# Second mixer: the weights' exact rests move from GpSimd to VectorE, and the skip is added straight out of PSUM

## The chip, the core and the metric

The kernel runs on one core of a Trainium2 chip. The metric is the device time of one execution in microseconds (us). The engines are called as in the profile: PE is TensorE (PEld its weight loads), DVE is VectorE, ACT is ScalarE, POOL is GpSimd, SP is SyncE, which issues nearly all DMAs.

## The reference, cut to what matters

Two decoder layers run one after the other on 512 tokens of width 1024. The change lies in the mixer of the second layer, a Mamba-2 state-space mixer with 32 heads of 64 channels in 4 groups:

```python
def mamba2_mixer(h, norm, w_in, conv_w, conv_b, dt_bias, a_log, d_skip, gnorm, w_out):
    proj = rms_norm(h, norm) @ w_in              # z | x,B,C | dt
    xbc = silu(causal_depthwise_conv(xbc, conv_w, conv_b))
    ...
    y = ssd_chunked(xf * dt[..., None], dt * A, b_in, c_in)   # inside a chunk + from the states
    y = y + xf * d_skip.astype(f32)[:, None]                  # the skip
    y = y.reshape(b, s, SSM_INNER) * silu(z)
    y = y * rsqrt(mean(y * y over a group) + eps) * gnorm
    return y @ w_out
```

## The kernel before

**Three passes for every product.** Weights and activations are float32. Each weight tile `wraw` (128 x 1024 values, one DMA of 512 KB) is split into a rounded part `whi` (a copy on ScalarE) and the exact rest `wlo = wraw - whi` (a `tensor_tensor` subtraction). A product is then three matmuls: `xh,whi`, `xl,whi` and `xh,wlo` (`mm3`). Which engine makes the rest is set by the list `lo_turns`, from which `wload3` takes turns: `[V]` is VectorE, `[G]` is GpSimd. The second mixer sets it to `[G]` at L1482 and back to `[V]` at L1728, before its last output product. There are two buffers each of `wraw`, `whi` and `wlo`, so a weight tile's DMA waits until an earlier tile's rest is made, and a rounded half waits until the matmuls are done with the one two tiles before.

**The second mixer.** `odd_mixer` works by groups of 8 heads. The generator `core(g, ...)` does a group's scan in steps; `weave` spreads the dense products (`dq`: the next group's projections, the previous group's output product, and for the last group the keys and values of the memory, `mem_kv`) evenly between its steps. A dense product of one weight tile is a "job" of 24 matmuls into one of three PSUM buffers `lin`; its `sink` takes the result out of PSUM: `pd` and then three multiply-adds and a gate into `xf`, `Bt`, `Ct` for the convolutions, or `z` for the gates, or an addition to `hT` for outputs.

In `core`, for each of four pairs of heads `hp`: `pst` (PSUM, one buffer) gets the states' part of chunks 1 to 3; `seg` is made by ScalarE (decays) and multiplied with `CB` on VectorE; `py` (PSUM) gets the part inside the chunks from `seg`; VectorE puts `y` together and multiplies it into `zs[hp]`. `ecums[hp]` holds the decays with which `pst` is scaled; it is a tile `ecumB` with two buffers, loaded by two DMAs on SP's queue in `cum_load`. After the four pairs, `gss` collects the sum of squares (added on GpSimd), and VectorE multiplies the four `z` with it and makes the split halves `oyh`, `oyl` for the output product.

**What sets the order.** The program is written in one order, and a scheduler then sets each engine's own order from a simulated timeline. Each engine runs its list strictly in that order. The changed program goes through the same scheduler.

Of the kernel before, what the change touches and what calls it, by code (L numbers as in the profile page):

```python
# [15 lines left out]
ALU = mybir.AluOpType  # L16
# [4 lines left out]
P = 128  # L21
T = 512
# [57 lines left out]
def kernel(ctx: ExitStack, tc: tile.TileContext, a: dict, out: bass.AP, stage: str = "exfoXF"):  # L80
    nc = tc.nc
    V, S, G, TE = nc.vector, nc.scalar, nc.gpsimd, nc.tensor
# [12 lines left out]
    def nm(s):  # L95
        uid[0] += 1
        return f"{s}_{uid[0]}"
# [12 lines left out]
    def ps(tag="ps", n="", w=512):  # L110
        p_, tags = next(c for c in reversed(cur) if tag in c[1])
        return p_.tile([P, w], F32, tag=tag, name=nm(n or tag), bufs=tags[tag])
# [3 lines left out]
    def mm(o, l, r, start, stop, **kw):  # L116
        last_mm[0] = TE.matmul(o, l, r, start=start, stop=stop, **kw)  # L117
# [3 lines left out]
    def act(o, i, f, scale=1.0, bias=0.0, **kw):  # L121
        ins = S.activation(o, i, f, scale=scale, bias=bias, **kw)  # L122
        if f in (AF.Silu, AF.Tanh, AF.Sin):
            switch.append(ins)
        return ins

    def logs():

        with ExitStack() as es:
            for ins in switch:  # L130
                es.enter_context(tc.issue_after(ins.ins))
            S.preload_act_table_set(LNS)
        switch.clear()

    def tt(e, o, x, y, op):
        return e.tensor_tensor(o, x, y, op=op)  # L136

    def stt(o, x, sc, y, op0, op1):
        return V.scalar_tensor_tensor(o, x, sc, y, op0=op0, op1=op1)  # L139
# [38 lines left out]
    lo_turns = [V]  # L178
# [43 lines left out]
    dcol = cp.tile([P, 16], F32, name="dcol")  # L222
# [102 lines left out]
    def rsq(o, src, scale, bias):  # L325
        act(o, src, AF.Ln, scale=scale, bias=bias)
        act(o, o, AF.Exp, scale=-0.5)
# [1151 lines left out]

    def odd_mixer():  # L1480
        win = a["od_w_in"][0]
        lo_turns[:] = [G]  # L1482
        wout = a["od_w_out"][0]
        INNER = 2048
        NC = T // P
# [6 lines left out]
        with pool("odd") as op, pool("oddram", space=DRAM) as dp, \  # L1492
                psum(lin=3, pc=2, py=2, ps2=1):
            xh, xl, R, fin = prenorm(xp, colr("od_norm", 8), tag="py")
            t_ = lambda tag, shape, bufs=1, dt=F32: op.tile(list(shape), dt, tag=tag, name=nm(tag), bufs=bufs)
# [102 lines left out]
            def core(g, d, zs, res):  # L1598
                Bt, Ct, xf = d["B"], d["C"], d["xf"]
                EL = t_("EL", (P, HG, NC), 2)  # L1600
                nc.sync.dma_start(EL, edram[g * HG:(g + 1) * HG, :].partition_broadcast(P))
                cums, ecums = [], []

                def cum_load(hp):
                    h0 = g * HG + hp * 2
                    cumB = t_("cumB", (P, 2, T), 2)
                    nc.sync.dma_start(cumB, cdram[h0:h0 + 2, :].partition_broadcast(P))
                    cums.append(cumB)
                    ecumB = t_("ecumB", (P, T - P), 2)
                    for j in range(2):  # L1610
                        nc.sync.dma_start(ecumB[j * 64:(j + 1) * 64, :], xdram[h0 + j, P:T].partition_broadcast(64))
                    ecums.append(ecumB)

                cum_load(0)
                BT = t_("BT", (P, NC, P))
                pt = ps("pc", "odd_m_pt2")
                for c in range(NC):
                    TE.transpose(pt[:, c * P:(c + 1) * P], Bt[:, c * P:(c + 1) * P], ident)
                act(BT.rearrange("p c n -> p (c n)"), pt, AF.Copy)
                CB = t_("CB", (P, NC, P))  # L1620
                pt = ps("pc", "odd_m_pt3")
                for c in range(NC):
                    cs = slice(c * P, (c + 1) * P)
                    mm(pt[:, cs], Bt[:, cs], Ct[:, cs], True, True)
                tt(V, CB, pt.rearrange("p (c l) -> p c l", c=NC), smask.unsqueeze(1).to_broadcast([P, NC, P]), ALU.mult)
                yield
                xdt = [t_(f"xdt{c}", (P, 512)) for c in range(NC)]
                sts = [None] * NC
                for c in range(NC):
                    cs = slice(c * P, (c + 1) * P)  # L1630
                    pt = ps("pc", "odd_m_pt4")
                    for i in range(4):
                        TE.transpose(pt[:, i * P:(i + 1) * P], xf[i][:, cs], ident)  # L1633
                    hb = lambda j: tms[:, j, c, g * HG:(g + 1) * HG].unsqueeze(2).to_broadcast([P, HG, 64])
                    ptv = pt.rearrange("p (h d) -> p h d", d=64)
                    tt(V, xdt[c].rearrange("p (h d) -> p h d", d=64), ptv, hb(0), ALU.mult)
                    if c < NC - 1:
                        xe = t_("xe", (P, 512), 2)
                        tt(V, xe.rearrange("p (h d) -> p h d", d=64), ptv, hb(2), ALU.mult)
                        pS = ps("pc", "odd_m_pS5")  # L1640
                        mm(pS, BT[:, c, :], xe, True, True)
                        st = t_(f"st{c}", (P, 512))
                        if c == 0:
                            act(st, pS, AF.Copy)
                        else:
                            eb = EL[:, :, c].unsqueeze(2).to_broadcast([P, HG, 64])
                            tt(G, st.rearrange("p (h d) -> p h d", d=64), sts[c].rearrange("p (h d) -> p h d", d=64),
                               eb, ALU.mult)
                            tt(V, st, st, pS, ALU.add)
                        sts[c + 1] = st  # L1650
                    yield
                ss = t_("gss", (P, T))
                for hp in range(4):

                    hs2 = slice(hp * P, (hp + 1) * P)
                    pst = ps("ps2", "odd_m_ps8")
                    for c in range(1, NC):
                        mm(pst[:, c * P:(c + 1) * P], sts[c][:, hs2], Ct[:, c * P:(c + 1) * P], True, True)
                    y = t_("y", (P, T), 2)
                    dc = dcol[:, g * 4 + hp:g * 4 + hp + 1]  # L1660
                    tt(V, y[:, P:T], pst[:, P:T], ecums[hp], ALU.mult)
                    V.tensor_scalar(y[:, 0:P], xf[hp][:, 0:P], dc, None, op0=ALU.mult)
                    stt(y[:, P:T], xf[hp][:, P:T], dc, y[:, P:T], ALU.mult, ALU.add)
                    py = ps("py", "odd_m_py6")
                    if hp < 3:
                        cum_load(hp + 1)
                    for j in range(2):
                        hl = hp * 2 + j
                        h = g * HG + hl
                        cB = cums[hp][:, j, :]  # L1670
                        sg = t_("seg", (P, NC, P), 2)
                        for c in range(NC):
                            act(sg[:, c, :], cB[:, c * P:(c + 1) * P], AF.Relu, scale=-1.0, bias=tms[:, 1, c, h:h + 1])
                        act(sg, sg, AF.Exp, scale=-1.0)
                        tt(V, sg, sg, CB, ALU.mult)
                        q2 = slice(j * 64, j * 64 + 64)
                        hs = slice(hl * 64, hl * 64 + 64)
                        for c in range(NC):
                            mm(py[q2, c * P:(c + 1) * P], xdt[c][:, hs], sg[:, c, :], True, True)
                        yield  # L1680
                    tt(V, y, y, py, ALU.add)
                    tt(V, zs[hp], y, zs[hp], ALU.mult)
                    if hp == 0:
                        act(ss, zs[hp], AF.Square)
                    else:
                        sq = t_("y", (P, T), 2)
                        act(sq, zs[hp], AF.Square)
                        tt(G, ss, ss, sq, ALU.add)
                yield
                pr = ps("pc", "odd_m_pr7")  # L1690
                mm(pr, ones, ss, True, True)
                Rg = t_("gss", (P, T))
                logs()
                rsq(Rg, pr, 1.0 / 512, eps_c)
                yield
                yh, yl = [], []
                for hp in range(4):
                    tt(V, zs[hp], zs[hp], Rg, ALU.mult)
                    h_ = t_(f"oyh{hp}", (P, T), dt=F32R)
                    l_ = t_(f"oyl{hp}", (P, T), dt=F32R)  # L1700
                    split(h_, l_, zs[hp], col("ssm_gnorm", g * 4 + hp))
                    yh.append(h_)
                    yl.append(l_)
                res.extend((yh, yl))
                yield
# [53 lines left out]
    if "o" in stage:  # L1759
        mem = odd_mixer()  # L1760
# [51 lines left out]
```

## Time and profile before

| | |
|---|---|
| time, median of 3 runs | 1826.12 us (1825.3 to 1826.51) |
| profiled execution | 1823.81 us, its span 1822.0 us |
| busy in the span | PE 96%, PEld 76%, DVE 61%, ACT 41%, POOL 21% |
| granted TensorE clock, mean | 0.978 of 2.4 GHz |

The span runs from the first to the last instruction of the profiled execution; 1.8 us lie around it. Busy time of PE counts matmuls from issue to modelled end, and they overlap, so PE counts as busy while one follows the other; what is read below is where PE is *not* busy and what ended that wait. The mixer of the second layer lies between about 930 and 1380 us of the span.

### The profile page before, as it was taken

To read this page: it belongs to the slowest core of one execution; us is meant where nothing else is said; L and a number is where in the kernel's file an instruction comes from. 1 tells how busy PE (TensorE), PEld (TensorE's weight loads), DVE (VectorE), ACT (ScalarE), POOL (GpSimd) and SP (SyncE) were. 2 spreads that over 40 slices of the span, in tenths; PEclk is the share of its full clock that TensorE was granted. 3 is DMA by queue.
4 is the path that set the end of the run, shared out by engine and by line. 5 is a ranking of instruction groups with operands and counts; after the bars stand their busy time and mean duration, and the time that the engine had idled before them with its cause. 6 is when DMAs were issued, how large, how long until landed. Compare 5 with 4: busy or idle time off the path is not lost. (4 is left out here: it accounts for less than half of the span.)

```text
span 1822.0 us, 25550 instructions
## 1 busy us (share of the span) xinstructions
PE 1746.2 (96%) x10192; PEld 1385.7 (76%) x10192; DVE 1111.7 (61%) x1662; ACT 741.5 (41%) x1273; POOL 382.1 (21%) x265
## 2 busy tenths in 40 slices
PE   7899999999899999999998998999989999999998
PEld 5667767777677888888875766777777788888886
DVE  6586677757566444343476979688776754443543
ACT  3443454455444223132354645454544432222322
POOL 6222211211312100001253344334341100000000
PEclk9899989999999999999999999999999999999999
DMA  5232101012212333333333423233332133323332
GB/s 158 70 90 83 48 19 29 21 59 82 81 35 93 94 103 94 98 97 95 93 93 105 122 80 122 71 118 97 90 116 70 47 104 95 102 93 100 97 93 93
DMA packets 171869, 157.15 MB, mean 86 GB/s; under 512 B 12075, under 2 KB 150182, under 8 KB 171750
## 3 DMA queue, kind: packets, MB, share of 16 engines
q1 hardware_dynamic: 169574, 155.51, 28.3%
q8 instruction: 80, 1.31, 0.3%
q14 instruction: 39, 0.32, 0.1%
q10 hardware_dynamic: 2176, 0.01, 0.1%
HBM read 150.90 MB, written 4.59 MB: 85 GB/s over the span
## 5 line engine op out<-in xcount | busy, mean ns | idle before, releaser
L122 ACT ACTIVATE whi<-wraw 128x1024 fp32r<-128x1024 f32 (+1 forms) x255 | 265.8, 1042 | 589.6 <-PE lin L117 498.6
L117 PE MATMUL lin<-xh,whi 128*128 128x512 f32 x1192 | 475.0, 401 | 10.8 <-ACT whi L122 5.0
L117 PE MATMUL lin<-xl,whi 128*128 128x512 f32 x1192 | 472.1, 397 | 1.0 <-DVE xl L139 1.0
L117 PE MATMUL lin<-xh,wlo 128*128 128x512 f32 x1192 | 453.9, 397 | 1.7 <-POOL pd L1553 1.2
L136 DVE TENSOR_TENSOR wlo<-wraw,whi 128x1024 fp32r<-128x1024 f32 (+1 forms) x158 | 193.9, 1227 | 339.5 <-ACT whi L122 339.2
L136 POOL TENSOR_TENSOR wlo<-wraw,whi 128x1024 fp32r<-128x1024 f32 x97 | 237.9, 2453 | 598.2 <-ACT whi L122 589.7
L117 PEld LDWEIGHTS lin<-xh,whi 128*128 128x128 f32 x1192 | 226.0, 190 | 63.6 <-issue 8.7
L117 PEld LDWEIGHTS lin<-xh,wlo 128*128 128x128 f32 x1192 | 225.5, 189 | 54.2 <-issue 2.4
L117 PEld LDWEIGHTS lin<-xl,whi 128*128 128x128 f32 x1192 | 225.8, 189 | 52.2 <-issue 2.1
L136 DVE TENSOR_TENSOR hT<-hT,lin 128x512 f32<-128x512 f32 x160 | 107.8, 684 | 82.9 <-PE lin L117 82.1
L117 PE MATMUL lin<-gl,whi 128*128 128x512 f32 x352 | 137.3, 390 | 0.5 <-DVE gl L136 0.5
L117 PE MATMUL lin<-gh,whi 128*128 128x512 f32 x352 | 136.2, 391 | 0.0
L117 PE MATMUL lin<-gh,wlo 128*128 128x512 f32 x352 | 125.7, 389 | 0.0
L136 DVE TENSOR_TENSOR s<-lin,R 128x512 f32<-128x512 f32 x88 | 60.0, 690 | 52.3 <-PE lin L117 52.3
L117 PEld LDWEIGHTS lin<-gl,whi 128*128 128x128 f32 x352 | 66.1, 188 | 14.4 <-DVE gl L136 0.9
L117 PEld LDWEIGHTS lin<-gh,wlo 128*128 128x128 f32 x352 | 66.1, 188 | 13.7
L117 PEld LDWEIGHTS lin<-gh,whi 128*128 128x128 f32 x352 | 66.1, 188 | 13.5
L122 ACT ACTIVATE s<-s 128x512 f32<-128x512 f32 x44 | 27.4, 624 | 69.0 <-DVE s L136 69.0
L122 ACT ACTIVATE seg<-cumB,tms 128x128 f32<-128x128 f32 x128 | 40.3, 390 | 31.0 <-PE odd_m_py L117 30.6
L117 PE MATMUL lin<-oyh,wlo 128*128 128x512 f32 x128 | 50.3, 398 | 1.7 <-DVE wlo L136 1.7
L117 PE MATMUL lin<-oyh,whi 128*128 128x512 f32 x128 | 51.8, 405 | 0.1
L117 PE MATMUL lin<-oyl,whi 128*128 128x512 f32 x128 | 51.2, 400 | 0.0
(440 smaller groups left out, 2854.3 us busy)
## 6 DMA issues: line engine op xcount, KB each, us to landing
wraw<-in_ffn_w_dram SPq DMA_DIRECT2D x176, 256.0 KB
wraw<-in_ffn_w_dram SPq DMA_DIRECT2D x44, 512.0 KB
wraw<-in_od_w_in_dram SPq DMA_DIRECT2D x41, 512.0 KB
wraw<-in_ev_w_in_dram SPq DMA_DIRECT2D x17, 512.0 KB
wraw<-in_xa_wkv_dram SPq DMA_DIRECT2D x16, 512.0 KB
cumB<-cdram SPq DMA_DIRECT2D x16, 512.0 KB
wraw<-in_od_w_out_dram SPq DMA_DIRECT2D x16, 512.0 KB
wraw<-in_ev_w_out_dram SPq DMA_DIRECT2D x8, 512.0 KB
```

The lines of the kernel that those rows point to most:

```text
L117: last_mm[0] = TE.matmul(o, l, r, start=start, stop=stop, **kw)
L122: ins = S.activation(o, i, f, scale=scale, bias=bias, **kw)
L136: return e.tensor_tensor(o, x, y, op=op)
```

## The change

Two edits, both in the second mixer. `lo_turns` is set to `[V]`, so that the 61 rests of this mixer that GpSimd made are made by VectorE (all but its last output product's, which VectorE made already). And `y` is put together in another way: before, `pst` was scaled into `y`, the skip (`xf` times a column of `dcol`) was written to `y`'s first chunk and added to the other three, and `py` was added. Now `pst` is scaled in place into the `ecumB` tile (`yst`), `y` is made in one step from `xf`, the column and `py` straight out of PSUM, and `yst` is added to chunks 1 to 3. That is three VectorE instructions per pair in place of four, and `y` is taken from its pool only after `py`.

```diff
     def odd_mixer():
         win = a["od_w_in"][0]
-        lo_turns[:] = [G]
+        lo_turns[:] = [V]
         wout = a["od_w_out"][0]
...
-                    y = t_("y", (P, T), 2)
-                    dc = dcol[:, g * 4 + hp:g * 4 + hp + 1]
-                    tt(V, y[:, P:T], pst[:, P:T], ecums[hp], ALU.mult)
-                    V.tensor_scalar(y[:, 0:P], xf[hp][:, 0:P], dc, None, op0=ALU.mult)
-                    stt(y[:, P:T], xf[hp][:, P:T], dc, y[:, P:T], ALU.mult, ALU.add)
+                    yst = ecums[hp]
+                    tt(V, yst, pst[:, P:T], yst, ALU.mult)
                     py = ps("py", "odd_m_py6")
...
-                    tt(V, y, y, py, ALU.add)
+                    y = t_("y", (P, T), 2)
+                    stt(y, xf[hp], dcol[:, g * 4 + hp:g * 4 + hp + 1], py, ALU.mult, ALU.add)
+                    tt(V, y[:, P:T], y[:, P:T], yst, ALU.add)
                     tt(V, zs[hp], y, zs[hp], ALU.mult)
```

Three places of VectorE's list show how the scheduler placed the rests. The first is the end of group 0's scan: `z<-z,gss` scales the four gates, `oyl` are the output's rests, and the last row takes the next group's first gate product out of a `lin` buffer. Before:

```order
L139 SCALAR_TENSOR_TENSOR xf_1618_8652<-pd_9282,colt,xf_1618_8652 128x512 x3
L139 SCALAR_TENSOR_TENSOR xf_1618_8652<-th_9289,xf_1618_8652 128x512
L136 TENSOR_TENSOR z_1609_8643<-z_1609_8643,gss_9214 128x512
L136 TENSOR_TENSOR z_1610_8644<-z_1610_8644,gss_9214 128x512
L136 TENSOR_TENSOR z_1611_8645<-z_1611_8645,gss_9214 128x512
L136 TENSOR_TENSOR z_1612_8646<-z_1612_8646,gss_9214 128x512
L139 SCALAR_TENSOR_TENSOR oyl_1730_9246<-z_1609_8643,colt,oyh_1729_9245 128x512
L139 SCALAR_TENSOR_TENSOR oyl_1732_9251<-z_1610_8644,colt,oyh_1731_9250 128x512
L139 SCALAR_TENSOR_TENSOR oyl_1734_9256<-z_1611_8645,colt,oyh_1733_9255 128x512
L139 SCALAR_TENSOR_TENSOR z_1739_9292<-lin_9337,R_8256 128x512
```

The same place on VectorE in the changed kernel:

```order
L136 TENSOR_TENSOR wlo_9379<-wraw_9331,whi_9378 128x1024
L139 SCALAR_TENSOR_TENSOR xf_1618_8652<-pd_9278,colt,xf_1618_8652 128x512
L139 SCALAR_TENSOR_TENSOR xf_1618_8652<-th_9285,xf_1618_8652 128x512
L136 TENSOR_TENSOR wlo_9427<-wraw_9382,whi_9426 128x1024
L136 TENSOR_TENSOR z_1609_8643<-z_1609_8643,gss_9210 128x512
L136 TENSOR_TENSOR z_1610_8644<-z_1610_8644,gss_9210 128x512
L136 TENSOR_TENSOR z_1611_8645<-z_1611_8645,gss_9210 128x512
L136 TENSOR_TENSOR z_1612_8646<-z_1612_8646,gss_9210 128x512
L139 SCALAR_TENSOR_TENSOR oyl_1730_9242<-z_1609_8643,colt,oyh_1729_9241 128x512
L139 SCALAR_TENSOR_TENSOR oyl_1732_9247<-z_1610_8644,colt,oyh_1731_9246 128x512
L139 SCALAR_TENSOR_TENSOR oyl_1734_9252<-z_1611_8645,colt,oyh_1733_9251 128x512
L139 SCALAR_TENSOR_TENSOR z_1739_9288<-lin_9333,R_8256 128x512
```

Two rests now stand ahead of the four scalings; the second one waits for a rounded half that ScalarE can write only when PE is done with the job two tiles before.

The second place is group 1's third and fourth pair on VectorE, where `seg` must be ready for PE's next `py`. Before:

```order
L136 TENSOR_TENSOR y_9755<-y_9755,odd_m_py_1837_9759 128x512
L136 TENSOR_TENSOR z_1741_9294<-y_9755,z_1741_9294 128x512
L136 TENSOR_TENSOR y_9875<-odd_m_ps_1855_9871,ecumB_9762 128x384
L1662 TENSOR_SCALAR y_9875<-xf_1618_8652,dcol 128x128
L136 TENSOR_TENSOR pd_9897<-lin_9847,R_8256 128x512
L139 SCALAR_TENSOR_TENSOR y_9875<-xf_1618_8652,dcol,y_9875 128x384
L139 SCALAR_TENSOR_TENSOR xf_1747_9300<-th_9838,xf_1747_9300 128x512
L136 TENSOR_TENSOR seg_9880<-seg_9880,CB_9316 128x512
L136 TENSOR_TENSOR hT_76<-hT_76,lin_9913 128x512
L136 TENSOR_TENSOR seg_9934<-seg_9934,CB_9316 128x512
```

The same place in the changed kernel:

```order
L136 TENSOR_TENSOR wlo_9898<-wraw_9836,whi_9897 128x1024
L139 SCALAR_TENSOR_TENSOR y_9857<-xf_1617_8651,dcol,odd_m_py_1836_9750 128x512
L139 SCALAR_TENSOR_TENSOR xf_1748_9297<-pd_9887,colt,xf_1748_9297 128x512
L136 TENSOR_TENSOR hT_76<-hT_76,lin_9903 128x512
L136 TENSOR_TENSOR y_9857<-y_9857,ecumB_9631 128x384
L139 SCALAR_TENSOR_TENSOR xf_1748_9297<-pd_9887,colt,xf_1748_9297 128x512
L139 SCALAR_TENSOR_TENSOR xf_1747_9296<-th_9829,xf_1747_9296 128x512
L136 TENSOR_TENSOR seg_9870<-seg_9870,CB_9312 128x512
L136 TENSOR_TENSOR z_1741_9290<-y_9857,z_1741_9290 128x512
L136 TENSOR_TENSOR seg_9924<-seg_9924,CB_9312 128x512
```

The fourth pair's skip is gone from the rows ahead of its `seg`; the third pair's sum out of `py`, two convolution steps and a rest have come there.

The third place is the chain of the memory's keys on VectorE: `nv`, `nt`, `nt`, `rk`, `k` is one key's norm, each from the one before. Before:

```order
L318 TENSOR_SCALAR nv_11545<-mem_k_pr_2187_11543 128x256
L136 TENSOR_TENSOR nt_11546<-rk_11540 128x256
L139 SCALAR_TENSOR_TENSOR nt_11546<-nt_11546,nv_11545 128x256
L139 SCALAR_TENSOR_TENSOR rk_11540<-nt_11546,rk_11540 128x256
L318 TENSOR_SCALAR nv_11597<-mem_k_pr_2198_11595 128x256
L139 SCALAR_TENSOR_TENSOR k_2146_11364<-kf_11538,gk_11367,rk_11540 128x256
```

And in the changed kernel:

```order
L318 TENSOR_SCALAR nv_11527<-mem_k_pr_2186_11525 128x256
L136 TENSOR_TENSOR wlo_11635<-wraw_11594,whi_11634 128x1024
L139 SCALAR_TENSOR_TENSOR k_2145_11347<-kf_11473,gk_11350,rk_11475 128x256
L136 TENSOR_TENSOR nt_11528<-rk_11522 128x256
L139 SCALAR_TENSOR_TENSOR nt_11528<-nt_11528,nv_11527 128x256
L139 SCALAR_TENSOR_TENSOR rk_11522<-nt_11528,rk_11522 128x256
L136 TENSOR_TENSOR wlo_11673<-wraw_11638,whi_11672 128x1024
L139 SCALAR_TENSOR_TENSOR k_2145_11347<-kf_11520,gk_11350,rk_11522 128x256
```

One rest stands in each key's chain now.

## Rows read from the trace of the kernel before

**Rows 1.** Stretches: us, then busy us (x count) of PE, PEld, DVE, ACT, POOL; PEclk, DMA share, GB/s.
```profile
600.00:900.00 300.00, 300.00 (x1325) 248.55 (x1324) 121.53 (x149) 82.72 (x96) 23.91 (x10) 1.00 0.32 97
...
940.00:1000.00 60.00, 51.54 (x222) 39.29 (x220) 45.16 (x55) 28.83 (x44) 20.05 (x15) 0.94 0.36 105
...
1060.00:1075.00 15.00, 10.46 (x46) 8.40 (x45) 12.21 (x15) 8.33 (x12) 4.88 (x2) 0.89 0.13 36
...
1120.00:1142.00 22.00, 16.08 (x76) 12.51 (x76) 19.61 (x21) 11.07 (x22) 8.72 (x6) 0.84 0.34 105
...
1318.00:1360.00 42.00, 35.08 (x236) 31.04 (x235) 32.43 (x39) 20.44 (x40) 21.77 (x10) 0.96 0.37 108
...
1000.00:1320.00 320.00, 309.04 (x1479) 241.34 (x1478) 257.86 (x311) 165.79 (x299) 129.60 (x75) 0.98 0.34 100
```

**Rows 2.** Waits of PE from 930 to 1380 us: us in total, times, longest us.
```profile
PE odd_m_py L117 <- DVE seg L136: 7.9, 4, 4.5
PE lin L117 <- DVE z L139: 4.5, 1, 4.5
PE odd_m_py L117 <- DVE xdt L136: 3.5, 1, 3.5
PE mem_k_pr L117 <- ACT ksq L122: 2.2, 2, 1.9
...
PE lin L117 <- DVE wlo L136: 1.7, 1, 1.7
PE lin L117 <- POOL pd L1553: 1.2, 1, 1.2
```

**Rows 3.** VectorE's groups, 940 to 1360 us: count | busy us, mean ns | idle before.
```profile
L139 DVE SCALAR_TENSOR_TENSOR xf<-pd,colt,xf 128x512 f32<-128x512 f32 x48 | 47.8, 1011 | 2.2 <-ACT xf L122 1.7
L136 DVE TENSOR_TENSOR seg<-seg,CB 128x512 f32<-128x512 f32 x32 | 36.3, 1148 | 3.6 <-ACT seg L122 3.6
L139 DVE SCALAR_TENSOR_TENSOR z<-th,z 128x512 f32<-128x512 f32 x16 | 27.9, 1747 | 9.8 <-ACT th L122 9.8
L139 DVE SCALAR_TENSOR_TENSOR y<-xf,dcol,y 128x384 f32<-128x384 f32 x16 | 23.2, 1451 | 0.0
L136 DVE TENSOR_TENSOR z<-z,gss 128x512 f32<-128x512 f32 x16 | 17.5, 1154 | 5.3 <-ACT gss L122 5.3
...
L139 DVE SCALAR_TENSOR_TENSOR z<-lin,R 128x512 f32<-128x512 f32 x16 | 11.0, 685 | 12.5 <-PE lin L117 8.9 <-DMA xdram<-z 3.5
...
L1662 DVE TENSOR_SCALAR y<-xf,dcol 128x128 f32<-128x128 f32 x16 | 8.9, 558 | 0.0
L136 DVE TENSOR_TENSOR y<-odd_m_ps,ecumB 128x384 f32<-128x384 f32 x16 | 8.8, 549 | 0.8 <-PE odd_m_ps L117 0.6
```

**Rows 4.** GpSimd and VectorE instructions in order of time: start us, us, engine, operation.
```profile
1132.98 2.79 POOL L136 TENSOR_TENSOR wlo<-wraw,whi 128x1024 fp32r<-128x1024 f32 x1
1133.49 2.82 DVE L136 TENSOR_TENSOR seg<-seg,CB 128x512 f32<-128x512 f32 x1
...
1330.63 2.40 POOL L136 TENSOR_TENSOR wlo<-wraw,whi 128x1024 fp32r<-128x1024 f32 x1 [0.67 <-ACT whi L122]
1330.73 2.57 DVE L139 SCALAR_TENSOR_TENSOR rk<-nt,rk 128x256 f32<-128x256 f32 x1
```

**Rows 5.** GpSimd's groups, 940 to 1360 us, columns as in group 3.
```profile
L136 POOL TENSOR_TENSOR wlo<-wraw,whi 128x1024 fp32r<-128x1024 f32 x56 | 140.0, 2500 | 137.2 <-ACT whi L122 128.8 <-PE odd_m_pt L1633 6.0 <-PE odd_m_ps L117 2.3
L136 POOL TENSOR_TENSOR gss<-gss,y 128x512 f32<-128x512 f32 x12 | 18.2, 1519 | 18.8 <-ACT y L122 18.8
L136 POOL TENSOR_TENSOR st<-st,EL 128x512 f32<-128x512 f32 x8 | 8.5, 1062 | 22.4 <-ACT st L122 11.8 <-DVE st L136 10.7
```

**Rows 6.** VectorE's rests in the first FFN, 640 to 900 us, columns as in group 3.
```profile
L136 DVE TENSOR_TENSOR wlo<-wraw,whi 128x1024 fp32r<-128x1024 f32 x40 | 48.9, 1224 | 122.5 <-ACT whi L122 122.5
```

**Rows 7.** SP's queue from 930 to 1380 us, waits: us in total, times, longest us.
```profile
SPq L1611 <- DVE y L136: 29.5, 7, 6.6
```

## Prediction

> **What bounds the kernel now.** I read first how the span splits into stretches. In the first FFN PE is busy for all of 300 us at a granted clock of 1.00 [rows 1]: nothing that VectorE does there costs time. In the second mixer PE is short of work in four places: 60.00 − 51.54 = 8.5 us from 940 to 1000, 4.5 from 1060 to 1075, 5.9 from 1120 to 1142 and 6.9 from 1318 to 1360, 25.8 us together [rows 1]. The granted clock falls there too. A stretch of t us at a mean clock c does work that full clock would do in c·t, so the clock costs 60 × 0.06 = 3.6, 15 × 0.11 = 1.7, 22 × 0.16 = 3.5 and 42 × 0.04 = 1.7, together 10.5 us. So 36 us is the most that this change can bring: all else is PE at work.
>
> Second, the list of what PE waits for between 930 and 1380 us: nearly all names VectorE (`seg` 7.9 us, `z` 4.5, `xdt` 3.5) [rows 2]. In the same stretches VectorE is busy 75 to 89% of the time (19.61 of 22 us from 1120 to 1142) [rows 1].
>
> Third, why VectorE is late: its instructions of one size have very different times [rows 3]. A 128x512 step out of PSUM, `z<-lin,R`, takes 685 ns; the same size with both inputs in SBUF takes 1011 (`xf`), 1148 (`seg`), 1154 (`z` by `gss`) or 1747 (`z<-th`). For 128x384, `y<-odd_m_ps,ecumB` out of PSUM takes 549 and the skip's step, all SBUF, 1451. Put in order of time, GpSimd and VectorE show the reason: `seg` starts 0.5 us into a GpSimd rest of 2.79 us and ends 0.54 us after it, that is, it runs its own time once the rest is over; a `rk` of half the size, started 0.1 us into a rest of 2.40, ends 0.27 after it [rows 4]. VectorE stands still while GpSimd reads.
>
> The Trainium skill, page "SBUF — State Buffer", section "Who interferes with whom", says the same: a VectorE instruction with two SBUF inputs and a GpSimd one that reads SBUF share a port that is locked for a whole instruction, and "Issue order, not op shape, decides who blocks". By that last sentence the moved rests would in turn hold GpSimd's remaining steps; that rival is weighed below by its rows.
>
> **The change part by part.** *Holds removed.* Excess over the PSUM forms [rows 3]: `xf` 48 × (1.011 − 0.685) = 15.6 us, `seg` 32 × 0.463 = 14.8, `z<-th` 16 × 1.062 = 17.0, the skip's step 16 × 0.902 = 14.4, `z` by `gss` 16 × 0.469 = 7.5: 69 us. GpSimd is busy with rests for 140.0 us of 166.7 in this stretch, the others being `gss` 18.2 and `st` 8.5 [rows 5], so 84%, 58 us, should go with the rests. Bounds: nothing, if the times are those of the forms and not of GpSimd (but `seg` and `xf` are of one size and differ, and [rows 4] shows ends tied to GpSimd's), and all 69.
>
> *Rests added.* A VectorE rest takes 1224 ns in the FFN [rows 6]; the 56 of this stretch [rows 5] make 68.5 us, the 61 of the mixer 75.
>
> *The sum of `y`.* Removed are 8.9 us (skip of the first chunk) and 23.2 us (its step on three) [rows 3], of which 14.4 are already counted as holds. The sum with `py` stays one step out of PSUM, now with the skip in it; the trace has no such form of three operands except `z<-lin,R` of 685 ns, which I take for it (bounds: 16 × (±0.2), 3 us). Added is a 128x384 step with both inputs in SBUF: 549 if free of GpSimd, 1451 if held as today; I take 549, 8.8 us, since the rests go. Net −8.9 − 8.8 + 8.8 = −8.9 us.
>
> So VectorE's load changes by −58 + 68.5 − 8.9 = +1.6 us of some 340: **no relief on average**. What changes is where it is. A hold of up to 2.8 us falls on whatever VectorE has next; where it is always busy, nearly the whole rest of 2.5 us is lost for each GpSimd rest, and in its place stands a step of 1.22 us. I go by stretch.
>
> 940 to 1000: the `xdt` wait (3.5) and `pd` (1.2) hang on held `z<-th` and `xf` steps. One `z<-th` hold of 1.1 and two or three `xf` of 0.33 lie in each such chain: I take 3 of 8.5 us.
>
> 1060 to 1075, the end of a group: the four scalings lose 4 × 0.47 = 1.9 us of holds, `xf` steps ahead of them some 2; by the order shown above, two rests have come ahead of the scalings, of which one, 1.22, comes out of this chain's time. Gain 3 of 4.5.
>
> 1120 to 1142: VectorE-bound over the two pairs before (`seg` waits, the longest 4.5 [rows 2]). Two pairs have four `seg` (1.9 us of holds), two skip steps (1.8) and `y`'s own saving (2 × 8.9/16 = 1.1), some six `xf` (2.0) and three `z<-th` (3.2): 10 us out, four rests in, 4.9. Gain 5 of 5.9.
>
> 1318 to 1360, the keys: each key's chain has a hold of about 2 us (`rk`, 2.57 us, ends 0.27 after the rest [rows 4]) and by the order gets one rest of 1.22 in its place; the last group's `seg` and scalings lose 1.5 + 1.9. I take 4 of 6.9.
>
> Sum 15 of 25.8 us. The clock comes back in proportion, 15/25.8 × 10.5 = 6 us; it was 0.84 where PE idled most and 1.00 where it never did [rows 1].
>
> *New waits.* VectorE now stands at a rest until `whi` is there, and `seg`, `xf`, `y` are queued behind it. Below: 0, as in the FFN, where VectorE sat idle 122.5 us ahead of 40 rests for `whi` [rows 6] and PE was never short. Above: the four stretches are 139 us of 420, so about 20 rests lie in them, each at 1.7 us, PE's one wait for a VectorE rest [rows 2]: 34 us. I take three waits of 1.7, one for each of the three stretches where VectorE is the engine waited for, 5 us, since elsewhere the FFN is the nearer row.
>
> *Moved.* The `ecumB` buffer is now free only after `yst` is added. The load that reuses it is issued by SP, which stands 29.5 us for it today, 7 times, up to 6.6 [rows 7], and none of PE's longer waits is for it [rows 2]; a pair takes over 20 us (16 pairs in some 380), so I cost it at nothing. Without that cover it would cost what lies between the two steps: about a rest, five 512 steps and a 384 step, 1.22 + 5 × 0.685 + 0.55 = 5.2 us, once a group, 21 us.
>
> Total −15 − 6 + 5 = −16 us: 1823.8 becomes 1807.8 for an execution like the profiled one, which lies 2.3 us below the median; so about 1810.
>
> **The rivals.** *Half comes back.* If holds only hide behind ScalarE (`th` 9.8 us, `seg` 3.6, `gss` 5.3 of VectorE's own waits [rows 3]), PE gets 7 or 8 us and with a little clock, less new waits, −8: 1818.
>
> *All comes back*: −36 to −30, 1790 to 1796. VectorE's unchanged mean load speaks against it.
>
> *GpSimd held in turn.* The 12 `gss` additions run on GpSimd at 1519 ns [rows 5]; if each rest on VectorE holds one up by its 1.22, the last of each group is on the chain to the scalings: 4 × 1.2 = 5 us, and 1815. This is what issue order deciding, in the Trainium skill's section named above, would give; no row of before shows a VectorE rest beside a GpSimd step. I count it within the forecast's range.
>
> *`ecumB` late*: the 21 us above; at 16 it eats the gain. Up to 1831. Against it: a whole pair's time as cover.
>
> *Slower: VectorE, in order, stands at its rests.* GpSimd idled 128.8 us for `whi` ahead of 56 rests, 2.3 us each [rows 5], and nobody was behind it. From 1000 to 1320 VectorE has 320 − 257.86 = 62 us free [rows 1] for some 43 of the rests, 1.44 us each: **from a mean standing time of 1.44 us on, VectorE is full** and becomes the bound. At 2.3 it lacks 43 × 0.86 = 37 us, less the 16 of gain: 1845. For it: the second rest ahead of the scalings waits for a job that PE has yet to finish. Against it: GpSimd idled because it was free early; a busy engine comes to a rest when `whi` has long been there.
>
> *The holds are not GpSimd's doing.* Then 68.5 us of rests come on top, 43 × 1.22 = 53 of them from 1000 to 1320, VectorE at 303 of 320 after `y`'s saving of 7.5: about 1835. [rows 4] speaks against it.
>
> **How the numbers follow.** Of 1826, 0.2% is 3.7 us, about what a measurement of this kernel can tell from no change: faster is below 1822.5. Forecast with its own range 1798 to 1815: 0.60. Half: 0.21. All: 0.05. `ecumB` late: 0.05, shared between no change and slower. VectorE standing: 0.06. No holds to remove: 0.03. Faster is 0.60 + 0.21 + 0.05 less 0.02 for the edge of the half case, 0.84; no change 0.02 + 0.03 = 0.05; slower 0.02 + 0.06 + 0.03 = 0.11. The range from 1796 to 1823 leaves out the slower cases and most of the full return.
>
> **What would show it.** Right: `xf`, `seg` and `z<-z,gss` near 0.7 us, `z<-th` under 1; VectorE's busy time within a few us of before, GpSimd's near 27 from 940 to 1360; PE's waits for `seg`, `z` and `xdt` together under 8 us; clock in 1120 to 1142 above 0.9. Wrong: VectorE idle for `whi` above 60 us with PE waits for `seg` behind it; `xf` still near 1 us; PE waiting for the states' loads.

## The result and the profile after

The changed kernel takes 1805.64 us (median of 5 runs, 1798.9 to 1808.38) against 1826.12: the ratio is 0.9887, with a 95% interval of 0.9868 to 0.9906. The forecast was 1810 us and a range from 1796 to 1823. The profiled execution took 1798.9 us, the shortest of the five; its span is 1797.1.

Single executions differ by some us ahead of the change already. The first FFN ends at 918.7 us in the trace of before and at 916.8 in the one after, with nothing changed until then; over the runs below that point lies between 916.7 and 923.3. So beside the medians I compare the length of **the second mixer in the trace**, from the end of the first FFN's last addition to `hT` to the end of the last but one of this mixer's: 1375.2 − 918.7 = 456.5 us before, 1350.9 − 916.8 = 434.2 after. Those 22.3 us answer to the 20.5 of the medians; the rest of the program is as long as before within a few us.

VectorE's groups after the change, from 940 to 1336 us (the same part of the program as in [rows 3]; columns as there):

```profile
L136 DVE TENSOR_TENSOR wlo<-wraw,whi 128x1024 fp32r<-128x1024 f32 x58 | 72.4, 1248 | 8.4 <-ACT whi L122 5.7 <-PE lin L117 2.3
L139 DVE SCALAR_TENSOR_TENSOR xf<-pd,colt,xf 128x512 f32<-128x512 f32 x46 | 37.6, 823 | 1.7 <-ACT xf L122 1.6
L136 DVE TENSOR_TENSOR seg<-seg,CB 128x512 f32<-128x512 f32 x32 | 21.1, 685 | 0.0
...
L139 DVE SCALAR_TENSOR_TENSOR y<-xf,dcol,odd_m_py 128x512 f32<-128x512 f32 x16 | 11.9, 745 | 7.4 <-PE odd_m_py L117 7.4
L139 DVE SCALAR_TENSOR_TENSOR z<-th,z 128x512 f32<-128x512 f32 x16 | 11.8, 740 | 0.4 <-ACT th L122 0.4
...
L136 DVE TENSOR_TENSOR z<-z,gss 128x512 f32<-128x512 f32 x16 | 10.0, 687 | 3.1 <-ACT gss L122 3.1
...
L136 DVE TENSOR_TENSOR ecumB<-odd_m_ps,ecumB 128x384 f32<-128x384 f32 x16 | 8.9, 554 | 2.0 <-PE odd_m_ps L117 1.9
L136 DVE TENSOR_TENSOR y<-y,ecumB 128x384 f32<-128x384 f32 x16 | 8.8, 552 | 0.1
```

`seg` fell from 1148 ns to 685, `z<-th` from 1747 to 740, `z` by `gss` from 1154 to 687, `xf` from 1011 to 823: what looked like slow forms in [rows 3] were mostly holds, that is, time in which the step stands still beside a GpSimd step. GpSimd has these reading steps left:

```profile
L136 POOL TENSOR_TENSOR gss<-gss,y 128x512 f32<-128x512 f32 x12 | 20.0, 1666 | 103.6 <-ACT y L122 103.6
L136 POOL TENSOR_TENSOR st<-st,EL 128x512 f32<-128x512 f32 x8 | 9.0, 1131 | 108.3 <-ACT st L122 81.1 <-DVE st L136 27.2
```

The stretches of [rows 1], now at the places where PE is as far in its work as at 940, 1000, 1060, 1075, 1120, 1142, 1318 and 1360 us before (columns as there):

```profile
938.00:997.00 59.00, 50.97 (x222) 39.39 (x221) 43.91 (x62) 29.74 (x45) 2.73 (x8) 0.91 0.34 99
1055.50:1068.50 13.00, 10.69 (x46) 8.51 (x45) 10.69 (x17) 7.20 (x11) 0.00 (x0) 0.87 0.15 42
1113.30:1125.70 12.40, 12.40 (x66) 10.06 (x65) 12.37 (x19) 8.52 (x17) 1.98 (x3) 1.00 0.45 144
1299.00:1335.80 36.80, 33.91 (x236) 30.35 (x236) 28.70 (x46) 21.77 (x42) 3.34 (x2) 0.95 0.42 126
```

The third row is the plainest: 22 us at a clock of 0.84, with PE waiting for `seg`, have become 12.4 us of PE without a gap at 1.00. The first has hardly changed.

These places are worked out from the starts of the matmuls in both traces: each counts as much as its kind's median distance to the next start in the trace of before, and times at which the sums are equal belong together. The same sums tell where the time came from:

| stretch before, us | its length before | after | gain | taken in the prediction, before new waits |
|---|---|---|---|---|
| 940 to 1000 | 60.0 | 59.1 | 0.9 | 3 + its share of 6 for the clock |
| 1000 to 1060 | 60.0 | 58.3 | 1.7 | 0 |
| 1060 to 1075 | 15.0 | 13.0 | 2.0 | 3 + share |
| 1075 to 1120 | 45.0 | 44.8 | 0.2 | 0 |
| 1120 to 1142 | 22.0 | 12.4 | 9.6 | 5 + share |
| 1142 to 1318 | 176.0 | 173.3 | 2.7 | 0 |
| 1318 to 1360 | 42.0 | 36.8 | 5.2 | 4 + share |

PE's waits after the change, from 925 to 1355 us, as in [rows 2]:

```profile
PE odd_m_pt L1618 <- DVE Bt L139: 5.6, 1, 5.6
PE lin L117 <- DVE z L139: 2.3, 1, 2.3
PE odd_m_pt L117 <- DVE Ct L139: 1.4, 1, 1.4
PE lin L117 <- ACT oyh L122: 1.2, 1, 1.2
PE odd_m_py L117 <- DVE xdt L136: 0.8, 1, 0.8
```

The 7.9 us for `seg` are gone; a wait of 5.6 us for `Bt` is new. Its cause stands in VectorE's timeline of the changed kernel (start us, us, instruction; in brackets the idle time before it and what ended it):

```profile
967.15 0.69 DVE L136 TENSOR_TENSOR xdt<-xdt,xdt 32x512 f32<-32x512 f32 x1
971.78 1.29 DVE L139 SCALAR_TENSOR_TENSOR z<-lin,R 128x512 f32<-128x512 f32 x2 [3.94 <-DMA xdram<-z]
972.98 0.74 DVE L139 SCALAR_TENSOR_TENSOR Ct<-pd,colt,Ct 128x512 f32<-128x512 f32 x1
973.64 0.69 DVE L139 SCALAR_TENSOR_TENSOR Bt<-th,Bt 128x512 f32<-128x512 f32 x1
```

The first gate's step may not write `z0` until the DMA to `xdram` has read it, since the exponentials `ecum` stand in the same buffer. That wait was there before (3.5 us, `DMA xdram<-z` in [rows 3]), but now `Bt`'s last step is queued behind it.

### The profile page after: what moved, and what is told of

It is laid out like the page before. It is cut to its first block, busy times and chain, and to the rows that moved or that the text cites. A ratio compares the mean times of both kernels' runs of the same rounds, so it can differ in the third digit from the quotient of the medians.

```text
span 1797.1 us, 25503 instructions
## 1 busy us (share of the span) xinstructions
PE 1733.4 (96%) x10192; PEld 1379.4 (77%) x10192; DVE 1087.6 (61%) x1707; ACT 742.9 (41%) x1273; POOL 232.8 (13%) x204
## 4 chain that ended last, share of the span: by engine, by line
PE 86%; DVE 6%; DMA 3%; ACT 3%; issue 1%; SPq 1%; ACTq 0%; DVEq 0%
PE lin L117 67%; PE xattn_q L117 2%; PE odd_m_py L117 2%; PE rw_x L117 1%; PE mla_sc L117 1%; DMA wraw<-in_ev_w_in_dram 1%; DVE xl L139 1%; PE rw_gram L117 1%; PE mla_q L117 1%; PE mla_pv L117 1%; PE mla_kv L117 1%; PE rw_y L117 1%; DVE wlo L136 1%; PE xattn_po L117 1%; PE mla_pT L1447 1%
## 5 line engine op out<-in xcount | busy, mean ns | idle before, releaser
L136 DVE TENSOR_TENSOR wlo<-wraw,whi 128x1024 fp32r<-128x1024 f32 (+2 forms) x219 | 270.1, 1233 | 355.3 <-ACT whi L122 352.3
L136 POOL TENSOR_TENSOR wlo<-wraw,whi 128x1024 fp32r<-128x1024 f32 (+1 forms) x36 | 85.8, 2382 | 452.4 <-ACT whi L122 452.4
L117 PEld LDWEIGHTS lin<-gh,whi 128*128 128x128 f32 x352 | 66.0, 188 | 13.6
```

## The experiments

**One half of the change alone.** In the first run only the list of the rests is changed, in the second only the sum of `y`:

```
e1_rests_only:   before.py with   -  lo_turns[:] = [G]   +  lo_turns[:] = [V]   (in odd_mixer)
e2_y_only:       the changed kernel with   -  lo_turns[:] = [V]   +  lo_turns[:] = [G]
```

> Half of the change: the rests on VectorE, y put together as before. Theory 1 (VectorE steps with two SBUF inputs stand still while GpSimd reads; the change removes these holds): xf near 0.8 us, seg near 0.69, the skip's 128x384 step falls from 1451 ns to 550-600; most of the gain is here, 1806 to 1813. Theory 2 (the gain comes from y's shorter sum, which needs py one step earlier): less than a third of the gain, 1819 to 1825.

> The other half: rests on GpSimd as before, y in the new form. Theory 1: xf stays near 1.0 us and seg near 1.15, the new addition of yst (two SBUF inputs) is held, 1.2 to 1.45 us for 128x384, while the sum out of PSUM takes 0.745 as after the change; VectorE is relieved of some 10 us, time 1818 to 1825. Theory 2: 1812 or less.

The rests alone: 1806.54 us, 0.9886 (0.9872 to 0.9899), as much as the whole change, and `seg` 819 ns, the skip's step 609. The sum of `y` alone: 1813.56, 0.9926 (0.9913 to 0.9938), between the two theories' figures and nearer to that of theory 2. Its VectorE rows, 940 to 1350 us:

```profile
L139 DVE SCALAR_TENSOR_TENSOR xf<-pd,colt,xf 128x512 f32<-128x512 f32 x48 | 48.8, 1032 | 5.7 <-ACT xf L122 5.1
L136 DVE TENSOR_TENSOR seg<-seg,CB 128x512 f32<-128x512 f32 x32 | 35.6, 1129 | 5.0 <-ACT seg L122 5.0
L139 DVE SCALAR_TENSOR_TENSOR z<-th,z 128x512 f32<-128x512 f32 x16 | 30.4, 1902 | 10.5 <-ACT th L122 10.5
...
L136 DVE TENSOR_TENSOR y<-y,ecumB 128x384 f32<-128x384 f32 x16 | 13.8, 862 | 0.2
...
L139 DVE SCALAR_TENSOR_TENSOR y<-xf,dcol,odd_m_py 128x512 f32<-128x512 f32 x16 | 11.9, 741 | 4.7 <-PE odd_m_py L117 4.7
```

The holds are still there (`z<-th` 1902 ns), but steps that could be held are fewer: gone are 23.2 + 8.9 us, come are 13.8 and 11.9 − 10.9 (the sum out of PSUM took 10.9 us before), 17.3 us less on these steps, since the addition of `yst` took 862 ns and not 1200 to 1450. Part of the holds moved to other steps (`z<-th` 1747 to 1902 ns, `xf<-th` 921 to 1098, `z<-y,z` 835 to 986): over the whole mixer VectorE is busy for 345.6 us where it was 352.9, 7.3 less, not far from the 10 that I had put. The time fell more than that relief let me expect: PE's gaps fell by 5.1 us (26.2 to 21.1), and the lower level of the clock lasts 10.2 us in the mixer instead of 20.5. PE's waits from 1000 to 1320 us, first of before, then of this run:

```profile
PE odd_m_py L117 <- DVE seg L136: 6.4, 3, 4.5
PE lin L117 <- DVE z L139: 4.5, 1, 4.5
```

```profile
PE odd_m_pS L117 <- DVE xe L136: 3.1, 1, 3.1
PE lin L117 <- POOL wlo L136: 1.2, 1, 1.2
PE odd_m_py L117 <- DVE seg L136: 1.1, 2, 0.6
```

The rests alone leave 1.4 us of the wait for `z` there and none for `seg`. So each half by itself removes most of the same waits, for `z` at a group's end and for `seg` in group 1, which fits that 20.6 and 13.6 us do not add up to more than 20.5. By the second group's end (the fourth `z` by `gss`, measured from the first FFN's end) the mixer is 8.5 us ahead with `y` alone and 10.6 with the rests alone; to its end `y` alone gains nothing more (8.6), the rests 17.9. The keys' chain has no `y` in it. Theory 2 falls: `y` is not needed for the gain, though it would have brought two thirds of it without the other edit. In the traces the mixer of the rests alone is 4.5 us longer than with both edits (438.7 and 434.2). The two are level at the third group's end (319.7 and 320.7 us); behind it PE waits 5.0 us for `kf` in the run of the rests alone and 1.3 with both. Whether `y`'s form or the scheduler's other order does that is not shown, and the medians, each good to some 3 us, cannot tell it.

**GpSimd made busy again.** Beside each rest of the second mixer, made on VectorE as in the changed kernel, GpSimd does a step whose result nobody reads, from `whi` (first run) or without reading (second run; these wait for nothing, so nearly all of them run ahead of the scan: the last of the 61 ends at 988.5 us, and only three begin behind the first `seg`). Both runs have the same order on the other engines, but for two neighbouring VectorE steps that change places ahead of the scan.

```
+   def reads(hi):
+       d_ = op.tile([P, 1024], F32, tag="dum", ...)
+       tt(G, d_, hi, hi, ALU.subtract)        # e3_gpsimd_reads
+       G.memset(d_, 0.0)                      # e4_gpsimd_writes, in its place
```

> The changed kernel, and beside each rest of the second mixer GpSimd subtracts whi from itself (128x1024) into a tile that nobody reads. No engine waits for it. Theory 1: VectorE is held again, seg and z by gss over 1.0 us, z<-th over 1.3, and now with the rests on VectorE on top: 1822 to 1850. Theory 3 (not holds, but that GpSimd's rests came late for PE and kept the weights' buffers long): VectorE's steps near 0.7 us and the time as after the change, 1799 to 1812.

> As the run with GpSimd's extra reads, in the same order on every engine, but GpSimd's extra step is a memset of the same tile: it writes and reads nothing. If reading is what holds VectorE: seg near 0.69, time as after the change, 1799 to 1812. If any busy GpSimd step holds it: as with the extra reads.

With reads: 1829.91 us, 1.0017 (1.0005 to 1.0029): all of the gain is gone, and a little more. With writes: 1805.54, 0.9880 (0.9865 to 0.9895): as the changed kernel. That time is no test of writes beside the scan, since the memsets were over before it; `seg` (684 ns) and `z<-th` (739) had next to no GpSimd step of this kind beside them. What the run shows of writes lies ahead of the scan and is read below. First VectorE's groups of the run with reads, 940 to 1370 us, and GpSimd's extra steps in it, then GpSimd's in the run with writes, 940 to 1345:

```profile
L136 DVE TENSOR_TENSOR wlo<-wraw,whi 128x1024 fp32r<-128x1024 f32 x59 | 95.4, 1619 | 8.4 <-ACT whi L122 8.2
L139 DVE SCALAR_TENSOR_TENSOR xf<-pd,colt,xf 128x512 f32<-128x512 f32 x48 | 53.5, 1119 | 0.5 <-ACT xf L122 0.3
L136 DVE TENSOR_TENSOR seg<-seg,CB 128x512 f32<-128x512 f32 x32 | 24.4, 787 | 0.0
L139 DVE SCALAR_TENSOR_TENSOR z<-th,z 128x512 f32<-128x512 f32 x16 | 22.8, 1426 | 0.4 <-ACT th L122 0.4
```

```profile
L136 POOL TENSOR_TENSOR dum<-whi 128x1024 f32<-128x1024 f32 x57 | 142.3, 2496 | 145.0 <-ACT whi L122 145.0
```

```profile
L1495 POOL MEMSET dum<- 128x1024 f32 x41 | 39.5, 963 | 2.1
```

`z<-th` is at 1426 ns again and `xf` at 1119; `seg` and `z` by `gss`, for which I expected over 1000, stayed at 787 and 767. The likely reason is that here GpSimd starts when VectorE's own rest does, and it is the rest that stands (1619 ns). PE pays for it: it waits for rests 9 times, 8.0 us in all. One place of the timeline of the run with reads shows hold and no hold side by side:

```profile
1106.67 1.90 POOL L136 TENSOR_TENSOR dum<-whi 128x1024 f32<-128x1024 f32 x1 [2.25 <-ACT whi L122]
1106.77 2.88 DVE L136 TENSOR_TENSOR wlo<-wraw,whi 128x1024 fp32r<-128x1024 f32 x1
...
1114.74 2.28 POOL L136 TENSOR_TENSOR dum<-whi 128x1024 f32<-128x1024 f32 x1 [2.30 <-ACT whi L122]
1115.46 0.56 DVE L136 TENSOR_TENSOR ecumB<-odd_m_ps,ecumB 128x384 f32<-128x384 f32 x1 [0.19 <-PE odd_m_ps L117]
```

The rest begins 0.1 us after GpSimd's step and ends 1.08 us behind it: it waited, then ran. The step out of PSUM, with one input in SBUF, runs its 0.56 us in the midst of GpSimd's. It is not always VectorE that stands. In another place of this run VectorE's steps came first:

```profile
1035.90 5.07 POOL L136 TENSOR_TENSOR dum<-whi 128x1024 f32<-128x1024 f32 x1 [1.54 <-ACT whi L122]
1036.19 0.68 DVE L136 TENSOR_TENSOR seg<-seg,CB 128x512 f32<-128x512 f32 x1
...
1039.13 2.38 DVE L139 SCALAR_TENSOR_TENSOR xf<-pd,colt,xf 128x512 f32<-128x512 f32 x1
```

GpSimd's step takes 5.07 us here, where 2.50 is the mean, while `seg` and three more steps of VectorE run their own time; only `xf` behind them is held. Of the seven `seg` steps that began inside a read in this run, five took 678 to 686 ns and two 2382.

In the run with writes VectorE's steps lie in the midst of memsets ahead of the scan:

```profile
952.92 2.98 POOL L1495 MEMSET dum<- 128x1024 f32 x3
953.11 1.23 DVE L136 TENSOR_TENSOR wlo<-wraw,whi 128x1024 fp32r<-128x1024 f32 x1 [0.18 <-ACT whi L122]
954.26 1.41 DVE L139 SCALAR_TENSOR_TENSOR xf<-pd,colt,xf 128x512 f32<-128x512 f32 x2
```

None of them stands. Ten `xf` steps that began inside a memset took 743 to 754 ns; twelve that began inside a read of the other run took 1543 to 2383. So reading holds VectorE and writing does not, as far as these steps show it. The Trainium skill, page "SBUF — State Buffer", section "Who interferes with whom", says that a VectorE step with two SBUF inputs contends with a GpSimd step that reads SBUF, "not with one that only writes it": the steps inside memsets and inside reads agree.

Nobody waits for what the extra steps write, so in the run with reads the time is not lost to rests that come late from GpSimd. The reads do keep `whi` longer; ScalarE stood for that once, 3.0 us at 933 us, ahead of the scan. And in the kernel before PE waited for a rest of GpSimd only once between 930 and 1380 us:

```profile
PE lin L117 <- POOL wlo L136: 1.2, 1, 1.2
```

Theory 3 falls.

**How much of the rests, and the last reading steps.** The rests by turns on both engines, `lo_turns[:] = [V, G]`; and the changed kernel with `gss` and `st` on VectorE (`tt(G, ss, ss, sq, ALU.add)` and `tt(G, st, ...)` with V). Beside them the changed kernel once more:

> The changed kernel as it is, for runs beside the others here. Theory 1 (holds by GpSimd's reads): 1803 to 1808 as before, PE's longest wait in the second mixer again some 5 us for Bt near 970 us.

> The changed kernel with the rests by turns on VectorE and GpSimd. Theory 1: about half of the holds (30 us) stay and half of the rests' 75 us are off VectorE; a hold comes unplanned and lasts up to 2.5 us, so it lies between the full move and y's new form alone (1813.6): 1806 to 1814. If VectorE's load were what counts, and not holds: under 1803.

> The changed kernel, and GpSimd's last reading steps in the scan, the 12 additions of gss and 8 of the states, are on VectorE too. Theory 1: the last 5 us of holds (xf from 820 ns to 747) go, 20 steps of some 0.69, 14 us, come; VectorE has some 100 us to spare, so 1802 to 1808. If GpSimd being held by VectorE in turn cost 5 us at the groups' ends (gss at 1.67 us where it was 1.52): 1799 to 1802.

The changed kernel again takes 1805.39 us, 0.9879 (0.9861 to 0.9896). Half of the rests: 1805.25, 0.9882 (0.9864 to 0.9900), no worse, though `xf` still takes 1017 ns, `seg` 959 and `z<-th` 1116. That is just under my 1806 to 1814, by less than the noise, and half of the holds seem to cost nothing. `gss` and `st` on VectorE: 1807.36, 0.9891 (0.9877 to 0.9906): `xf` is at 748 ns, the last holds are gone, and nothing is won. Nor does GpSimd being held in turn cost the 5 us of that rival: after the change `gss` takes 1666 ns, 1519 before, but the last one of each group, on which the scalings hang, is 0.65 us longer for all four groups together.

**The first stretch.** `ecum` in the idle buffer of `gss` (first run), and in addition ScalarE's last step for `Ct` ahead of the first decays (second run); the third is the second with half of the rests on GpSimd:

```
-                ecum = i_("z0")
+                ecum = i_("gss")                                    # e5, x1, x2
+                                if g == 0 and hp == 0:
+                                    es.enter_context(tc.issue_after(ct_th[0].ins))   # x1, x2
                                 act(sg[:, c, :], cB[...], AF.Relu, ...)
```

> The changed kernel, but the exponentials that go out to xdram stand in the buffer of gss, idle until the scan, and not in that of the first gate z0. After the change VectorE, in order, stands 3.9 us at the first gate's step until that DMA has read z0, and Bt's last step, for which PE then waits 5.6 us, is queued behind it. Theory A (this old wait, moved ahead of Bt by the new order, ate the gain of the first stretch): the wait for xdram is gone, PE's wait for Bt falls under 2 us, the time by 4 to 9 us against the changed kernel, to 1797 to 1802. Theory B (the first stretch is set by the weights' rests or by the decays' loads that ScalarE waits for, 4.4 us): PE's idle time only moves to its next wait, within 2 us of the changed kernel.

> The run with the own buffer for the exponentials, and ScalarE does the last step for Ct ahead of the first pair's decays; before, that step stood behind a decay that waited 4.7 us for the load of cumB, and PE 4.6 us for Ct. Theory B (two queued waits, one behind the other, hold the first stretch of the second mixer; each alone only passes PE's idle time on): PE's waits for Bt and Ct fall from 7.3 to some 3 us, the mixer from 434.8 us to 428 to 432, the time 1800 to 1804. Rival C (the round trip of the decays through DRAM sets the first stretch, and PE waits for seg or xdt instead): the mixer within 2 us of 434.8, time 1805 to 1807.

> The same with the rests by turns on VectorE and GpSimd. The half move took the same time as the full one although it keeps half of the holds (xf 1017 ns, seg 959), so beyond some point VectorE's time is not what sets the end. If so: as the run with both waits mended, within 2 us, with PE's idle time elsewhere. If the two kinds of loss add up now that the first stretch is shorter: 3 to 6 us slower than that run.

The own buffer: 1806.90 us, 0.9898 (0.9882 to 0.9915), the mixer 434.8 us, as the changed kernel when it ran again (434.8). PE's first three waits in it:

```profile
PE odd_m_pt L117 <- DVE Ct L139: 4.6, 1, 4.6
PE odd_m_pt L1618 <- DVE Bt L139: 2.7, 1, 2.7
PE lin L117 <- DVE z L139: 2.3, 1, 2.3
```

The wait for `xdram` is gone and `Bt` came earlier, but 4.6 us for `Ct` took its place: theory A fell, and the time is within 2 us of the changed kernel, as its theory B had it. With both mended: 1802.98 us where before took 1823.42 on the same chip, 0.9888 (0.9873 to 0.9903), the mixer 433.6 us:

```profile
PE odd_m_pt L1620 <- DVE Bt L139: 2.7, 1, 2.7
PE lin L117 <- DVE z L139: 2.3, 1, 2.3
PE odd_m_pt L1635 <- ACT BT L122: 1.7, 1, 1.7
PE odd_m_py L117 <- DVE xdt L136: 1.6, 1, 1.6
```

The idle time only moved on to `BT` and `xdt`, behind the decays, for whose load (`cumB`) ScalarE still stands 4.1 us. Theory B of this run fell too: the mixer should have come to 428 to 432 us, and the 1802.98 us lie in its range only because this chip was 2.4 us faster before the change as well. Rival C, the round trip of the decays through DRAM, fits; it was not tried by itself. Half of the rests on top: 1801.61, 0.9879 (0.9862 to 0.9895), the mixer 431.7 us, within 2 us of the run without it, as expected. None of these versions can be told from the changed kernel by its ratio.

| run | median us | ratio to before | second mixer, us | PE idle in it, us |
|---|---|---|---|---|
| before | 1826.12 | | 456.5 | 26.2 |
| changed | 1805.64 | 0.9887 | 434.2 | 13.2 |
| rests only | 1806.54 | 0.9886 | 438.7 | 17.0 |
| `y` only | 1813.56 | 0.9926 | 447.9 | 21.1 |
| GpSimd reads | 1829.91 | 1.0017 | 459.4 | 28.9 |
| GpSimd writes, nearly all ahead of the scan | 1805.54 | 0.9880 | 436.6 | 15.3 |
| half of the rests | 1805.25 | 0.9882 | 437.8 | 15.4 |

The last column is the sum of PE's gaps over 0.2 us in the profiled execution.

## Why the prediction was right, point by point

**The holds** were the cause, as forecast: the rests alone bring the whole gain, and the run with GpSimd's reads takes all 20 us back, with VectorE's steps held beside its reads (`xf` 1543 to 2383 ns) and not beside memsets (743 to 754). The bound "nothing" for them falls, and so does the rival that they were not GpSimd's doing.

**VectorE's load** was to change by +1.6 us. The rests took 1248 ns each (1224 taken), and VectorE is busy for 325.26 us of the 430 from 925 to 1355 us, where it was 347.44 of the 453 from 927 to 1380: 22 us less, over a stretch that holds the same work but for its edges. The term that was too small is the hold: 69 us were counted on five groups, of which I let 58 go. `seg`, `z<-th` and `z` by `gss` came down by 14.8 + 16.1 + 7.5 us, nearly all that was counted on them; `xf` came down by 9.0 of 15.6 (its own time is 748 ns, not the 685 that I had taken for it, and `gss` and `st` still hold it), and others that I had left out (`z<-y,z` 835 to 686 ns, `xf<-th` 921 to 752, the keys' `k` 1431 to 478) came down too.

**The sum of `y`.** 8.9 us net were put on it and their share counted in the gain of 1120 to 1142. VectorE saved 7.3 us of them (these steps take 28.0 us with the rests alone and 20.7 with both), but on top of the moved rests they bring no time that the medians show (1806.54 without, 1805.64 with). Alone they are worth 13.6 us. The step that failed here is adding both edits' savings where one wait is all that either can remove.

**The stretches.** 1120 to 1142 gave 9.6 us, more than the 5 + 2 taken: PE has no gap left there, and the whole stretch runs at the higher level of the clock. The keys gave 5.2, the group's end 2.0 for 3 + 1. The first stretch gave 0.9 for 3 + 2: the step that failed is "I take 3 of 8.5 us", for which I looked there for holds in front of `xdt` and `pd`. The waits for these two fell from 4.7 us to 0.8, but `Bt` and `Ct` came with 7.0 in their place. Taking away the old wait for `xdram` in front of `Bt` did not shorten the mixer either (434.8 us); what sets this stretch stays open, with rival C the one that fits. 4.4 us came from 1000 to 1060 and 1142 to 1318, where PE's gaps were 0.5 us in all before and I had taken 0. So the 36 us that I called the most this change can bring were no bound. Gaps shorter than the modelled end of a matmul don't show there as idle; whether that is where these 4.4 us were is not shown.

**The clock** was to give 6 us. In the mixer the records show 20.5 us at the lower of the two levels before and 17.1 after. Of these 2.5 and 4.4 us lie in PE's gaps, where they cost nothing; half of the rest is lost, 9.0 and 6.3 us: 2.7 came back. The 6.8 us at the lower level in 1120 to 1142 are gone, but in the first stretch, where PE now stands 5.6 us at a time, the lower level lasts 10.2 us instead of 6.8. "In proportion" was the wrong rule; what counted was which gaps closed.

**New waits** were put at 5 us for rests. VectorE stood 5.7 us for `whi` before 58 rests, 0.1 us each, and none of PE's waits in the scan names a rest: the bound of 0 was the right one, and the slower rival, which needed 1.44 us each, far off. The new wait that did come, 5.6 us for `Bt`, is of the size taken and of another cause: that the term came out right is luck.

**`ecumB`**: SP stood 13.5 us for `y` (9 times, up to 4.5) where it was 29.5 [rows 7] (with 20.4 more at the same loads for the skip's step of the first chunk, a row that I had not counted), and PE never for the load. Costing it at nothing was right.

In sum, −15, −6 and +5 were taken; the mixer's 22.3 us fall into 13.0 of PE's gaps (26.2 to 13.2), 2.7 of clock, and 6.6 that show in neither. So the mechanism was right, and that −16 came near the measured −20.5 is in part luck: the clock gave less than half of its term, and the 6.6 us for which I had no term made up for it.

## What to carry to other kernels

Before reading a long VectorE instruction as a slow form, look for the same size out of PSUM: here 0.69 us against 1.0 to 1.7, and most of the excess was GpSimd reading at the same time. Work moved off GpSimd can shorten the engine that receives it; taking one input from PSUM protects a step in the same way. Two edits that relieve the same wait are not to be added up: run each alone, and once most of PE's waits for the relieved engine are gone, half of the move may do (1805.25 us with half of the rests).

## What was not expected of the hardware

The engine that took over 70 us of work became 22 us less busy. Half of the holds may stay without a cost (`xf` 1017 ns, 1805.25 us). And writing did not hold VectorE where reading did: `xf` steps begun inside a 128x1024 memset of GpSimd (963 ns) took 743 to 754 ns, those begun inside a subtraction of that size 1543 to 2383. What writes all through the scan would cost was not measured.
